# A new order of the first three periods, and 18 casts and copies on the other engine, in a hand-ordered fast matrix multiplication

## The chip, the cores and the metric

One core of a Trainium2 chip. The metric is the device time of one execution in microseconds (us). Five engines run their own queues of instructions side by side: TensorE (PE in the profile; its weight loads are PEld), VectorE (DVE), ScalarE (ACT), GpSimd (POOL) and SyncE (SP), which here issues every DMA. Semaphores order them against each other.

## The reference

```python
def setup_inputs():
    B, S, D = 8, 2048, 2048
    return {"x": randn(B, S, D), "w": randn(D, D)}          # float32

def reference(x, w):
    cs = np.cumsum(x, axis=1)
    diff = cs - np.concatenate([zeros, cs[:, :-1, :]], axis=1)
    return np.matmul(diff, w).astype(np.float32)
```

The differences of a running sum are x again, so the result is the product of x, read as 16384 rows of 2048, with w, 2048 x 2048. The kernel computes that product.

## The kernel before

The 16384 rows are 128 tiles of 128. Tiles 0 to 3 are multiplied plainly, in bf16, while w arrives. Tiles 4 to 127 go in groups of four (two "g" and two "h" tiles) by the Strassen-Winograd scheme: seven products of half-sized blocks in place of eight. Inside a group the products P1 to P5 are again done by seven quarter-sized products where the class `Quarters` is used (methods `one` to `four`, `middle`, `last`, and `slot(i)` for the i-th product), and plainly where `Whole` is used. Row tiles are scaled to fp16 ("narrow", with "weigh", "mean", "scale" and "unit" for the scale), transposed by DMA ("turn") and combined on VectorE ("S1g" and the like); w is scaled into blocks B11, B12, B21, B22 and combined into T1 to T4, and these into the operands of the inner products ("in1" to "in5").

**Periods.** Period 0 is everything up to and with the first group (`group_plain`, tiles 4 to 7); period 1 is `group` for tiles 8 to 11, period 2 for tiles 12 to 15, and so on to period 30; period 31 is the tail.

**The order is written out by hand.** No operation is issued where the code names it. `record(label, engine, ask)` collects it; `emit(places)` at the end sorts all 6670 of them by `period * 1620 + place`, where `places` is a dictionary from label to a number for periods 0, 1, 2, 29, 30 and 31, and one shared by all other periods, and issues them. `after` ties each instruction to the one before it on its engine, so the sorted order is each engine's queue order. A place may be negative: an operation of period 1 with place -1416 sorts among those of period 0. Waits between engines come from the data: a reader waits for its writer, and a writer for the readers of what it overwrites.

**The start** (period 0, labels as in the code). `first x.q.r` (256 KB each, line 254) and `w.h.ko` (512 KB each, line 295) are loaded through SyncE's queue. `cast x.q.a` makes x bf16 (line 260), `turn x.q.a` transposes it on TensorE by eight 128x128 operations into one PSUM bank (line 269), `turned x.q.a` copies that to SBUF (line 279). `turn x.0.0` uses bank 6 and every other one bank 7, so each of these waits until the bank was copied out. `cast w.h.ko` makes w bf16 in a ring of seven buffers (line 313), and `max w.h.ko` takes its largest magnitude (line 305). `plain.h.r.ko` are the products of row tile r with that w (line 324; two matmuls of 128x512, one for row tile 3 in half 0). `part.0` to `part.4` (line 376) and `part` (line 421) are that tile's other columns for ko below 5; `left over` (line 476) finishes them later from B11 and B21. `out.h.r.n` copies a result to SBUF (lines 340 and 342) and `put out...` stores it. 30 dummies `warm.0` to `warm.29` (line 362) multiply zeros before data is there; the zeros lie where `turned x.0.0` writes later. When all of w is in, `max`, `max of all`, `uw` and `uinv` give its scale, and the blocks `B11.k`, `B21.k` (line 460 on VectorE) and `B22.k` (line 462 on ScalarE) are scaled; `T1.k` is line 543.

**The groups.** `load`, `weigh` (line 140), `mean` (161), `scale` (163), `unit` (167), `narrow` (178) and `turn` (195) prepare a row tile. `keep C..` (line 624, ScalarE) copies a product out of PSUM with its scale into one of four result buffers, `C..+P..` (line 635, VectorE) adds to it, and `put` (line 643) stores it, which frees the buffer. `P1.first`, `P1.out2`, `P1.out4` and their like are copies by ScalarE (line 627), and all other sums are VectorE's (line 576). Matmuls are line 588 (a whole group of four) and line 610 (inner products).

In the code that the change replaces, the engine of an operation is fixed by its line: `cast x` on VectorE; `cast w`, `narrow`, `part`, `keep` and the copies on ScalarE; `turned` and `out` by an argument or a name. Which products of group 8 and later are inner sevens is decided by `all_seven(g)`, true from tile 12 on.

## Time and profile before

| | us |
|---|---|
| median of 3 runs | 1449.7 (1449.27 to 1450.26) |
| span of the profiled execution | 1449.2 |
| TensorE busy | 1438.6 |
| VectorE busy | 1334.3 |
| ScalarE busy | 1204.5 |
| GpSimd busy | 0.5 |

The span runs from the first to the last instruction of the profiled execution. A line of the timeline gives start and length in us, engine, source line, operation, tile written<-tiles read, shape, count of merged instructions, and in brackets the idle time of that engine just before and what ended it. A line by stage gives the stretch, its length, and for each engine its busy time and instruction count, then TensorE's granted clock, the mean busy share of the 16 DMA engines and the GB/s moved. SyncE's own line (SPq) shows the issue of DMAs, not their landing.

### The profile page before, as it was taken

To read this page: it belongs to the slowest core of one execution; us is meant where nothing else is said; L and a number is where in the kernel's file an instruction comes from. 1 tells how busy PE (TensorE), PEld (TensorE's weight loads), DVE (VectorE), ACT (ScalarE), POOL (GpSimd) and SP (SyncE) were. 2 spreads that over 40 slices of the span, in tenths; PEclk is the share of its full clock that TensorE was granted. 3 is DMA by queue.
4 is the path that set the end of the run, shared out by engine and by line. 5 is a ranking of instruction groups with operands and counts; after the bars stand their busy time and mean duration, and the time that the engine had idled before them with its cause. 6 is when DMAs were issued, how large, how long until landed. Compare 5 with 4: busy or idle time off the path is not lost.

```text
span 1449.2 us, 20358 instructions
## 1 busy us (share of the span) xinstructions
PE 1438.6 (99%) x6692; PEld 652.2 (45%) x6698; DVE 1334.3 (92%) x2345; ACT 1204.5 (83%) x1994; POOL 0.5 (0%) x5
## 2 busy tenths in 40 slices
PE   8999999999999999999999999999999999999998
PEld 4444444444444444444444444444444444444443
DVE  6999999999999999999999999999999999999988
ACT  5997888898888888888988888988888888889783
POOL 0000000000000000000000000000000000000000
PEclk9999999999999999999999999999999999999999
DMA  9999979899888999989998888998989998989973
GB/s 360 369 252 272 252 212 228 240 247 262 226 234 226 243 262 231 244 222 228 247 265 233 228 229 237 252 257 226 222 239 244 260 248 225 218 236 248 264 200 116
DMA packets 343930, 351.59 MB, mean 243 GB/s; under 512 B 270992, under 2 KB 270992, under 8 KB 343824
## 3 DMA queue, kind: packets, MB, share of 16 engines
q1 hardware_dynamic: 343824, 350.29, 89.4%
q8 instruction: 52, 0.85, 0.2%
q14 instruction: 54, 0.44, 0.1%
HBM read 150.99 MB, written 134.22 MB: 197 GB/s over the span
## 4 chain that ended last, share of the span: by engine, by line
PE 91%; issue 4%; DMA 2%; ACT 2%; DVE 1%; DVEq 0%; POOLq 0%; ACTq 0%; SPq 0%
PE b L610 61%; PE b L588 30%; DMA x<-F 1%; DMA F<-in_x_dram 1%; DVE W L460 1%; ACT waste L140 0%; DMA out_dram<-arena 0%; ACT W L462 0%; DVE arena L635 0%; ACT arena L624 0%; ACT F L178 0%; ACT arena L342 0%; ACT arena L178 0%; DVE arena L576 0%; DVE W L576 0%
## 5 line engine op out<-in xcount | busy, mean ns | idle before, releaser
L588 PE MATMUL b<-W,x 128*128 128x512 f16 x2144 | 518.1, 379 | 0.1
L635 DVE SCALAR_TENSOR_TENSOR arena<-b,tiny,arena 128x512 f32<-128x512 f32 x612 | 446.9, 745 | 16.0 <-PE b L610 4.8
L610 PEld LDWEIGHTS <-arena 128*128 128x128 f16 x2744 | 268.2, 98 | 325.4 <-DVE arena L576 6.3
L610 PE MATMUL b<-W,arena 128*128 128x512 f16 x1672 | 413.7, 379 | 0.8 <-DVE arena L576 0.4
L624 ACT ACTIVATE arena<-b,tiny 128x512 f32<-128x512 f32 x496 | 317.0, 684 | 35.4 <-PE b L588 14.9
L588 PEld LDWEIGHTS <-x 128*128 128x128 f16 x2144 | 209.7, 98 | 253.3 <-issue 0.3
L140 ACT ACTIVATE waste<-F,tiny 128x1024 uint8<-128x1024 f32 x246 | 283.9, 1154 | 15.6 <-DMA F<-in_x_dram 14.1
L178 ACT ACTIVATE F<-F,tiny 128x1024 f16<-128x1024 f32 x246 | 282.1, 1147 | 10.9 <-DVE tiny L163 9.4
L610 PE MATMUL b<-W,x 128*128 128x512 f16 x1192 | 287.5, 379 | 0.0
L610 PE MATMUL b<-arena 128*128 128x512 f16 x1072 | 261.6, 379 | 0.0
L610 PEld LDWEIGHTS <-x 128*128 128x128 f16 x1428 | 139.7, 98 | 168.5
L576 DVE TENSOR_TENSOR b<-b,arena 128x512 f32<-128x512 f32 x298 | 205.9, 691 | 5.7 <-ACT arena L627 2.0
L627 ACT COPY b<-b 128x512 f32<-128x512 f32 x149 | 85.5, 574 | 134.4 <-PE b L610 112.4
L627 ACT COPY arena<-b 128x512 f32<-128x512 f32 x298 | 170.2, 580 | 19.9 <-PE b L610 13.0
L576 DVE TENSOR_TENSOR arena<-W 128x2048 f16<-128x2048 f16 (+1 forms) x158 | 185.6, 1176 | 0.4 <-PE b L610 0.4
L576 DVE TENSOR_TENSOR arena<-x,x 128x512 f16<-128x512 f16 (+1 forms) x181 | 91.5, 506 | 50.1 <-PE b L610 50.1
L576 DVE TENSOR_TENSOR x<-x,x 128x1024 f16<-128x1024 f16 x124 | 85.2, 687 | 2.0
L576 DVE TENSOR_TENSOR arena<-W,arena 128x512 f16<-128x512 f16 (+1 forms) x157 | 85.9, 563 | 0.6 <-PE b L610 0.5
L576 DVE TENSOR_TENSOR arena<-arena 128x512 f16<-128x512 f16 x120 | 50.8, 424 | 13.7 <-PE b L610 11.8
L610 PE MATMUL b<-arena,x 128*128 128x512 f16 x236 | 60.3, 379 | 0.0
L324 PE MATMUL b<-arena 128*128 128x512 bf16 x234 | 53.5, 379 | 1.5 <-DVE arena L279 0.8
L576 DVE TENSOR_TENSOR arena<-x,arena 128x512 f16<-128x512 f16 x119 | 49.6, 417 | 0.6 <-PE b L610 0.6
(49 smaller groups left out, 503.6 us busy)
## 6 DMA issues: line engine op xcount, KB each, us to landing
F<-in_x_dram SPq DMA_DIRECT2D x246, 512.0 KB, 5.4
out_dram<-arena SPq DMA_DIRECT2D x240, 512.0 KB, 4.8
W<-in_w_dram SPq DMA_DIRECT2D x31, 512.0 KB, 9.5
out_dram<-arena SPq DMA_DIRECT2D x31, 256.0 KB, 2.7
W<-in_x_dram SPq DMA_DIRECT2D x16, 256.0 KB, 6.6
x<-F SPq DMA_TRANSPOSE x246, 4.4
arena<-in_x_dram SPq DMA_DIRECT2D x2, 512.0 KB, 5.1
W<-in_w_dram SPq DMA_DIRECT2D x2, 256.0 KB, 9.0
```

The lines of the kernel that those rows point to most:

```text
L140: lambda: nc.scalar.activation(waste, data, ABS, bias=least, scale=1.0 / ROW, accum_out=m),
L178: lambda: nc.scalar.activation(to, data, COPY, scale=s),
L324: said = nc.tensor.matmul(to[n], xP[:, r, ko, :], b[:, ds(n * NB, NB)], start=(ko == 0), stop=(ko == KO - 1),)
L460: ask = lambda: nc.vector.tensor_scalar(to, src, uinv, None, MUL)
L576: record(label, "dve", lambda: nc.vector.tensor_tensor(dst, p, q, op))
L588: said = nc.tensor.matmul(to[n], a[k], b[k][:, n, :], start=(start and k == 0), stop=(k == KH - 1), skip_group_check=True,)
L610: said = nc.tensor.matmul(to, a[k], b[k], start=(start and k == 0), stop=(k == 3), skip_group_check=True)
L624: record(label, "act", lambda: nc.scalar.activation(c, p, COPY, scale=u))
L627: record(label, "act", lambda: nc.scalar.copy(to, p))
L635: label, "dve", lambda: nc.vector.scalar_tensor_tensor(c, p, u, c, MUL, ADD)
```

## The change

The same operations are recorded, 6670 of them, with the same 6698 matmuls. Three things change.

1. **Places.** The dictionaries for periods 0, 1 and 2 are new; those of 29, 30, 31 and of all other periods are the same. TensorE's, VectorE's, ScalarE's and SyncE's queues are the same again from the last operations of period 2 on.
2. **Engines.** 18 operations go to the other engine, listed in `moved`. In period 0, from VectorE to ScalarE: `cast x.0.1`, `cast x.1.0`, `cast x.1.1`, `cast x.2.1`, `cast x.3.0`, `turned x.0.0`, `out.0.1.0`. From ScalarE to VectorE: `cast w.0.0`, `w.0.1`, `w.0.5`, `w.0.6`, `w.0.7`, `w.1.1`, `turned x.3.1`, `out.0.0.1`, `out.1.2.1`, and in period 2 `P3.first` and `narrow6.1`.
3. **Code around it.** `all_seven` becomes `plainly(name, g)`, and the making of inner operands goes through `made`; with the settings here the same products stay inner or plain as before.

Queues at the start, before:

```
PE:  warm.0-21, turn x.0.1, warm.22-28, turn x.1.0, warm.29, turn x.0.0, plain.0.1.0, plain.0.0.0, ...
DVE: zeros, least, ones, ..., cast x.0.1, turned x.0.1, cast x.1.0, cast x.0.0, cast x.1.1, turned x.0.0, max w.0.0, ...
ACT: cast w.0.0, turned x.1.0, cast w.0.1, cast w.0.2, cast w.0.3, cast w.0.4, turned x.1.1, ...
SP:  x.0.2, x.1.1, x.0.0, x.1.3, x.0.3, x.0.1, x.1.2, x.1.0, w.0.0, w.0.1, x.2.3, w.0.2, w.0.3, ...
```

and after:

```
PE:  warm.0-27, turn x.0.1, turn x.0.0, warm.28-29, turn x.1.0, plain.0.0.0, plain.0.1.0, plain.0.0.1, ...
DVE: ones, zeros, ..., cast x.0.0, least, cast w.0.0, turned x.0.1, cast w.0.1, max w.0.2, max w.0.3, ...
ACT: cast x.0.1, cast x.1.0, turned x.0.0, cast w.0.2, turned x.1.0, cast x.1.1, cast w.0.3, turned x.1.1, ...
SP:  x.1.1, x.0.1, x.0.2, x.0.3, x.0.0, x.1.0, w.0.0, w.0.1, w.0.2, x.1.3, x.1.2, w.0.3, w.0.4, w.0.6, ...
```

ScalarE's queue where period 1 begins, before and after (operations of period 1 marked):

```
before: ... P2.first(1), keep C21.1#2, weigh7.1, mean7, narrow7.0, narrow7.1, P2.out2(1), unit7, keep C21.0#2,
        weigh4.0(1), unit5, P2.out4(1), keep C11g.1(1), keep C11g.0(1), keep C11h.1(1), weigh4.1(1), mean4(1), keep C11h.0(1), ...
after:  ... P2.first(1), unit4, weigh7.0, weigh7.1, mean7, keep C21.0#2, narrow7.0, P2.out2(1), keep C21.1#2, narrow7.1,
        keep C11g.0(1), P2.out4(1), keep C11g.1(1), weigh4.0(1), keep C11h.0(1), unit7, keep C11h.1(1), weigh4.1(1), mean4(1), ...
```

The diff, cut to its core:

```diff
+    moved = {
+        0: (
+            "turned x.0.0", "cast w.0.0", "cast x.0.1", "cast w.0.1", "cast x.1.0",
+            "cast x.1.1", "cast x.2.1", "cast w.0.5", "cast w.0.6", "cast w.0.7", "cast x.3.0",
+            "turned x.3.1", "cast w.1.1", "out.0.0.1", "out.0.1.0", "out.1.2.1",
+        ),
+        2: (
+            "P3.first", "narrow6.1",
+        ),
+    }
+
     def record(label, engine, ask):
...
+        if isinstance(ask, dict):
+            if label in moved.get(period[0], ()):
+                engine = {"act": "dve", "dve": "act"}[engine]
+            ask = ask[engine]
         ops.append((period[0], label, engine, ask))
+
+    def on_two(to, src, scale=None):
+        if scale is None:
+            return {
+                "act": lambda: nc.scalar.copy(to, src),
+                "dve": lambda: nc.vector.tensor_copy(to, src),
+            }
+        return {
+            "act": lambda: nc.scalar.activation(to, src, COPY, scale=scale),
+            "dve": lambda: nc.vector.tensor_scalar(to, src, scale, None, MUL),
+        }
...
-        record(f"cast x.{q}.{a}", "dve", lambda: nc.vector.tensor_copy(to, src))
+        record(f"cast x.{q}.{a}", "dve", on_two(to, src))
...
-        record(f"cast w.{h}.{ko}", "act", lambda: nc.scalar.copy(to, src))
+        record(f"cast w.{h}.{ko}", "act", on_two(to, src))
...
     places = {
         0: {
-            'first x.0.2': 0, 'first x.1.1': 1, 'first x.0.0': 2, 'first x.1.3': 3,
-            'first x.0.3': 4, 'first x.0.1': 5, 'first x.1.2': 6, 'first x.1.0': 7, 'w.0.0': 8,
...
+            'ones': 1, 'first x.1.1': 1, 'zeros': 2, 'first x.0.1': 2, 'numbers': 3, 'warm.0': 3,
+            'first x.0.2': 3, 'numbers turned': 4, 'warm.1': 4, 'first x.0.3': 4, 'eye': 5,
...
```

More of the change, by code (lines that the diff above doesn't have):

```diff
@@ L277, in turned @@
         v = v.rearrange("p (r c) -> p r c", r=2)
-        on = nc.scalar.copy if engine == "act" else nc.vector.tensor_copy
-        record(f"turned x.{q}.{a}", engine, lambda: on(to, v))
+        record(f"turned x.{q}.{a}", engine, on_two(to, v))
     wb = {}
@@ L420 @@
                 part(k)
-            record("part", "act", lambda: nc.scalar.copy(partial, banks[7]))
+            record("part", "act", on_two(partial, banks[7]))
     for ko in range(KO - KQ, KO):
@@ L815, in slot, with plainly, made @@
                 matmuls(*halves_of(f"{self.name}{name}", to, a, self.right, True)[at % 4])
+    def plainly(name, g):
+        return name in {PLAIN + 4: ('P1',)}.get(g, ())
+    making = {}
+    def made(name, inner, how):
+        if name not in making:
+            making[name] = True
+            how(inner)
     def group_plain(g):
@@ L972, in group @@
         P1.slot(1)
-        if more:
+        if not P1.plain:
             in_1.give("Q4")
@@ L1015, in group @@
         P1.slot(6)
-        if not more:
-            make_5(in_5)
-        in_5.give("Q3")
+        if not P5.plain:
+            made("P5", in_5, make_5)
+            in_5.give("Q3")
         C11h = keep("keep C11h", Y, uh, free.pop(1))
@@ L1033, in group @@
         total("S4g", S4g, A12g, S2g, SUB)
-        if not more:
-            make_1(in_1)
+        if not plainly("P1", g + 4):
+            made("P1", in_1, make_1)
+        if not plainly("P2", g + 4):
+            made("P2", in_2, make_2)
         go(2)
@@ L1055, in group @@
         P5.slot(4)
-        in_3.give("Q1")
+        if not P3.plain:
+            in_3.give("Q1")
         P5.last()
@@ L1101, in group @@
         P3.last()
-        in_4.give("Q1")
+        if not P4.plain:
+            in_4.give("Q1")
         scale_of(next_k)
@@ L1162, in group @@
         P4.slot(6)
+        if P4.plain and not plainly("P4", g + 4):
+            made("P4", in_4, make_3)
+        if P5.plain and not plainly("P5", g + 4):
+            made("P5", in_5, make_5)
+        if P3.plain and not plainly("P3", g + 4):
+            made("P3", in_3, make_3)
         turn(next_l, [1])
```

70 lines of the change are left out of this document (33 added, 37 removed), and 460 rows, old and new, of the table places.

## The prediction

> **What bounds the kernel now.** I read the page's first part, then busy time by stage, then the timeline of the stages that the change touches. From the page:
>
> ```profile
> span 1449.2 us, 20358 instructions
> PE 1438.6 (99%) x6692; PEld 652.2 (45%) x6698; DVE 1334.3 (92%) x2345; ACT 1204.5 (83%) x1994; POOL 0.5 (0%) x5
> ```
>
> The span is 1449.2 us and the median of the runs 1449.7, so 0.5 us lies around the span; sums are made in the span and the 0.5 added at the end. TensorE is busy for 99%. By stage (start:end, length, busy time of PE, PEld, DVE, ACT and POOL with instruction counts, clock, DMA share, GB/s):
>
> ```profile
> 0.00:13.20 13.20, 9.56 (x55) 4.49 (x55) 6.24 (x16) 2.91 (x3) 0.19 (x4) 1.00 0.82 284
> 13.20:41.00 27.80, 27.54 (x153) 13.53 (x157) 21.48 (x21) 22.14 (x25) 0.00 (x0) 1.00 1.03 405
> 41.00:118.00 77.00, 76.20 (x350) 34.15 (x352) 75.69 (x120) 68.57 (x100) 0.35 (x1) 1.00 1.01 304
> 118.00:146.00 28.00, 27.16 (x126) 12.05 (x124) 26.39 (x61) 22.93 (x40) 0.00 (x0) 1.00 1.02 258
> 146.00:1400.00 1254.00, 1254.00 (x5811) 568.17 (x5810) 1162.46 (x2061) 1064.45 (x1789) 0.00 (x0) 1.00 0.90 238
> ```
>
> From 146 to 1400 us PE has no idle time at all: 1254.00 us for 5811 matmuls, 0.2158 each. The change touches the first three periods, which end early in this last stage, and issues the same matmuls, so it can win only what PE idles before 146 us: 3.64 in the first stage (much of it the first load's latency), then 0.26, 0.80 and 0.84. In return any wait that the new order puts in front of PE costs its full length. A matmul's record is 0.379 long while the next follows after 0.216, so an idle time that the view prints is 0.16 shorter than the delay behind it; I add 0.16 below.
>
> **Part 1, the start.** Rows of the timeline (start, length, engine, line, operation, count, idle time before it and what ended it):
>
> ```profile
> 1.17 6.24 PE L362 MATMUL b<-arena 128*128 128x512 bf16 x22 [1.17 <-DVE arena L237]
> 8.34 0.69 DVE L260 CAST W<-W 128x1024 bf16<-128x1024 f32 x1 [5.08 <-DMA W<-in_x_dram]
> 9.09 0.62 PE L269 MATMUL b<-waste,W 128*128 128x128 bf16 x8 [1.68 <-DVE W L260]
> 9.55 1.68 PE L362 MATMUL b<-arena 128*128 128x512 bf16 x7
> 9.75 0.69 DVE L279 COPY arena<-b 128x1024 bf16<-128x1024 bf16 x1 [0.72 <-PE b L269]
> 10.37 1.90 DVE L260 CAST W<-W 128x1024 bf16<-128x1024 f32 x3
> 11.57 1.05 ACT L313 CAST arena<-W 128x1024 bf16<-128x1024 f32 x1 [9.57 <-DMA W<-in_w_dram]
> 12.52 1.01 ACT L279 COPY arena<-b 128x1024 bf16<-128x1024 bf16 x1
> 13.19 4.30 PE L324 MATMUL b<-arena 128*128 128x512 bf16 x17 [0.79 <-DVE arena L279]
> 16.09 1.04 ACT L313 CAST arena<-W 128x1024 bf16<-128x1024 f32 x1 [0.23 <-DMA W<-in_w_dram]
> 17.37 1.04 ACT L313 CAST arena<-W 128x1024 bf16<-128x1024 f32 x1 [0.23 <-DMA W<-in_w_dram]
> ```
>
> The two casts that end on DMA at 16.09 and 17.37 show the pace of loads: 1.28 per 512 KB tile, 0.64 per x block of half that size. Before, w.0.0 is the ninth load, behind eight x blocks, and lands just ahead of the cast at 11.57. After, it is the seventh, behind six: 1.28 earlier, so its cast can start at 10.29. That cast goes to VectorE (0.69 in row 8.34, against 1.05 on ScalarE) and ends at 10.98; `turned x.0.1` waits behind it in VectorE's queue and ends about 0.69 later, 11.67. `turn x.1.0` needs the PSUM bank that this copy empties: 11.74, with 0.45 for its eight transposes, and `plain.0.0.0` starts at 12.2. The other branch is earlier: `cast x.0.1` on ScalarE ends near 8.8 (its later block is the fourth load instead of the fifth: 8.34 less 0.64, plus 1.05), the 28 leading dummies end near 8.5 (row 1.17's end plus six of 0.216), `turn x.0.0` (behind `cast x.0.0`, 8.34 + 0.69, and `turn x.0.1`) and two more dummies end near 10.3, and `turned x.0.0` on ScalarE, 1.01, by 11.4. So the first product moves from 13.19 to 12.2: **gain 1.0**. The dummies themselves cost nothing: all lie before data is there.
>
> **Part 2, 13 to 41 us.** PE now runs ahead of the loads.
>
> ```profile
> 24.33 4.60 DVE L305 TENSOR_REDUCE tiny<-W 128x1 f32<-128x1024 f32 x4 [0.70 <-DMA W<-in_w_dram]
> 41.84 4.48 PE L324 MATMUL b<-arena 128*128 128x512 bf16 x19 [0.34 <-ACT arena L313]
> ```
>
> The reduction at 24.33 waits for the 20th load (w.0.8), after 7 MB. In the new order the 20th load, after the same 7 MB, is w.0.7. Its cast, on VectorE, ends at 24.33 + 0.69 = 25.0. PE needs it for `plain.0.3.7`: 52 matmuls (11.2) and two sets of transposes (0.9) behind 12.2 make 24.3. A wait of 0.8 appears, with about 0.2 more from the other tiles. The idle of the same stage before is 27.80 - 27.54 = 0.26 as printed, and up to 0.16 more for each wait in it: I take 0.7 for several short ones, between 0.26 and 0.9, and let it go. Net **-0.3**. The wait of 0.34 + 0.16 at 41.84, for `cast w.1.1` on ScalarE, goes too: that cast moves to VectorE and its tile comes one place earlier: **+0.5**. Ahead by 1.2 at 42 us.
>
> The 18 engine moves in themselves: an SBUF cast costs 0.69 on VectorE and 1.05 on ScalarE, `turned` 0.69 and 1.01 (rows 9.75 and 12.52); the two `out` copies about 0.1 more on VectorE than on ScalarE, by these rows:
>
> ```profile
> 40.27 0.58 ACT L342 COPY arena<-b 128x512 f32<-128x512 f32 x1
> 40.52 0.68 DVE L340 COPY arena<-b 128x512 f32<-128x512 f32 x1
> ```
>
> No row has `P3.first` (PSUM to PSUM) or `narrow6.1` on VectorE. The nearest are the subtraction from PSUM to PSUM and the scaling of SBUF:
>
> ```profile
> L627 ACT COPY b<-b 128x512 f32<-128x512 f32 x149 | 85.5, 574 | 134.4 <-PE b L610 112.4
> L576 DVE TENSOR_TENSOR b<-b,arena 128x512 f32<-128x512 f32 x298 | 205.9, 691 | 5.7 <-ACT arena L627 2.0
> L178 ACT ACTIVATE F<-F,tiny 128x1024 f16<-128x1024 f32 x246 | 282.1, 1147 | 10.9 <-DVE tiny L163 9.4
> 61.04 2.74 DVE L460 TENSOR_SCALAR W<-W,tiny 128x1024 f16<-128x1024 f32 x4
> ```
>
> I take 0.69 and, from the pace of row 61.04, 0.75: +1.4 of VectorE's time in period 2. From 146 us on VectorE has 1254.00 - 1162.46 free, 7%, so 20 us absorb it. Cost 0; the ends are 0 and +1.4 if it all meets PE. The Trainium skill ("VectorE: DVE Perf Modes", Specifications) puts VectorE closer to SBUF and ScalarE closer to PSUM, by which all four PSUM reads that go to VectorE would lose; the trace agrees for f32 (0.68 against 0.58) and not for bf16 `turned` (0.69 against 1.01). By the page the sum would be under 1 us worse on an engine with that slack, and the same on PE.
>
> **Part 3, 41 to 118 us.** All of w must be there before B11 is scaled, so this start is set by loads, not by PE:
>
> ```profile
> 56.69 2.96 ACT L313 CAST arena<-W 128x1024 bf16<-128x1024 f32 x3 [0.31 <-DMA W<-in_w_dram]
> 69.07 0.81 PE L476 MATMUL b<-W,arena 128*128 128x512 f16 x3
> 86.10 1.25 PE L588 MATMUL b<-W,arena 128*128 128x512 f16 x5 [0.25 <-DVE arena L576]
> ```
>
> The cast at 56.69 waits for w.1.13; w.1.14 follows 1.28 later, 57.9, last in both orders. So the scaling that starts at 61.04 stays there or comes up to 0.7 earlier, if VectorE is less behind with its reductions. `left over.0` comes 1.2 earlier, 67.9, and `A11g B11.0.0` at 68.5; B11.0 is now eleventh of the blocks and ready at 61.04 + 10 x 0.66 + 0.07 + 0.75 = 68.5: just in time. At 86.10 PE waits for `S1g` (0.25 + 0.16). In the new order two T2 blocks fall behind `S1g` and one `out` ahead of it, 0.6 sooner, while PE comes 1.2 sooner: the wait becomes 0.2 to 1.0, by how early the scaling starts; I take 0.3, since the reductions of w.0 all fit in VectorE's early gaps (21.48 busy of 27.80 in stage two). **+0.1**, and 0.1 more from smaller waits. Ahead by 1.4 at 118 us.
>
> **Part 4, 118 to 146 us.** This is where the sum is open.
>
> ```profile
> 129.72 0.58 ACT L627 COPY arena<-b 128x512 f32<-128x512 f32 x1 [0.48 <-PE b L610]
> 131.00 1.84 ACT L624 ACTIVATE arena<-b,tiny 128x512 f32<-128x512 f32 x3 [0.70 <-DMA out_dram<-arena]
> 132.97 1.03 PE L610 MATMUL b<-arena,x 128*128 128x512 f16 x4
> 133.35 1.15 ACT L140 ACTIVATE waste<-F,tiny 128x1024 uint8<-128x1024 f32 x1 [0.51 <-DMA F<-in_x_dram]
> 136.99 1.02 PE L610 MATMUL b<-W,arena 128*128 128x512 f16 x4 [0.40 <-ACT b L627]
> 138.45 1.90 PE L610 MATMUL b<-W,arena 128*128 128x512 f16 x8 [0.44 <-DVE arena L576]
> ```
>
> Before, ScalarE waits at 133.35 for load8.1 with `keep C11h.0` behind it; that delays VectorE's `C11h+P2.h`, and PE waits 0.56 and 0.60. After, `keep C11h.0` is ahead of that `weigh4.1`, so these 1.16 go. But `keep C11g.0`, which at 131.00 waits for a store (put3.1) to free its buffer, is now ahead of `P2.out4` (129.72) in ScalarE's queue. Behind `P2.out4` stand `P2.6` on PE and, on VectorE, `P2.last`, `S2g` and `S1h`. With the store at 131.0, `P2.out4` would end at 131.0 + 0.57 + 0.58 = 132.1. `P2.6` (132.97) stands one group of four (0.86) earlier in the new order and PE is 1.4 ahead: 130.7, a wait of 1.4. `P2.last` (0.69) and `S2g` (0.68) come only then, while PE has one group to do: 0.9 with the reaction times; `S1h` and the P5 sums behind them make 0.7 more. About 3.0. If the store lands by 129, `P2.out4` ends by 130.2 and only 0.3 of the last is left. It stands one place earlier in SyncE's queue (before load8.0), which is worth one tile, 1.28; so I take a landing near 130 and a wait of 1.6. Net 1.16 - 1.6 = **-0.4**, between +0.9 and -1.8.
>
> Sum: 1.0 - 0.3 + 0.5 + 0.1 + 0.1 - 0.4 = 1.0. After 146 us PE and VectorE find their old order again by period 3; I book 0. Span 1448.2, time **1448.7**.
>
> **The rivals.**
>
> *The store lands early.* Nothing takes the place of the 1.16: 1.4 + 0.9 = 2.3, so 1447.4. For it: the store's earlier place. Against it: at its end the rate of this stretch falls to what one DMA engine of 16 moves, and one instruction fetch lies in it; I read this as the fetch holding one engine back, and the fetch comes again.
>
> ```profile
> GB/s 197 262 131 229 295 197 262 328 262 229 197 197 229 295 229 295 328 328 328 426 426 360 361 338 391 369 340 246 272 240 207 172 137 104 72 33 45 33 33 33
> q8 instruction: 1, 0.02, 1.5%
> ```
>
> These are 127 to 132 us: the rate sinks from 426 to 33, a thirteenth. The Trainium skill ("Runtime: NRT & Kernel Launch", Instruction fetch mechanics) calls the cost of a fetch mostly hidden; by that the store lands without delay and this rival is right. Chance 0.27.
>
> *Every wait goes*, also w.0.7's and S1g's: 2.3 + 1.0 + 0.3 = 3.6, 1446.1. It needs loads faster than the rows show; chance 0.10.
>
> *Slower: ScalarE's queue behind the store.* Place: `keep C11g.0` ahead of `P2.out4`. Price: 3.0 at a landing of 131.0, and 1 us for each later. At 131.0 the sum is 1.4 + 1.16 - 3.0 = -0.4, 1450.1; it decides from a landing of 130.6. For slower by more than 0.2% (2.9 us) the store must land after 133.5. Chance 0.18 in all, 0.08 beyond 2.9.
>
> *It does not start earlier*: the first loads set the pace whatever the order, `plain` starts at 13.19 again and the rest nets to zero: 1449.7. Chance 0.10; the seventh place of w.0.0 speaks against it.
>
> **How the numbers follow.** Forecast 1448.7, chance 0.35; the others 0.27, 0.10, 0.18 and 0.10. A measurement of this kernel tells about 0.2% (2.9 us: 1446.8 to 1452.6) from no change. Faster by more: the "every wait goes" case and a little of the early store, 0.13. Slower by more: 0.08 from the store. Within: 0.79. The range of 8 in 10 takes in the early store, half of "every wait goes" and the store at 132: 1446.4 to 1451.2.
>
> **What would show it.** Right: L324's first matmul near 12.2; a PE wait near 25 ended by a VectorE cast; none at 41.8; ScalarE's L624 after 125 us with a wait on out_dram and PE idle right after it; no idle from 146 us. Wrong: first L324 at 13 or later, idle time of PE in periods 1 and 2 ended by VectorE (P3.first, narrow6.1), or PE idle near 68.5 for B11.

## The result, and the profile after

The changed kernel takes 1455.64 us (median of 5 runs, 1453.49 to 1457.7) against 1450.26 (1449.27 to 1450.42) for the kernel before beside it: the ratio is 1.0035, 95% interval 1.0023 to 1.0047. It is slower by 0.2 to 0.5%, and its runs spread over 4 us, those of the kernel before over 1.

The first part of the page after:

```profile
span 1452.6 us, 20366 instructions
PE 1439.5 (99%) x6691; PEld 652.6 (45%) x6698; DVE 1336.9 (92%) x2349; ACT 1201.0 (83%) x1990; POOL 0.5 (0%) x5
```

The work of every engine is the same within 4 us; the span is 3.4 longer. So the time has to be looked for where TensorE waits. By stage, after:

```profile
41.00:118.00 77.00, 74.85 (x344) 33.52 (x346) 74.60 (x115) 66.67 (x97) 0.35 (x1) 1.00 1.03 300
118.00:146.00 28.00, 28.00 (x131) 12.74 (x130) 27.81 (x67) 22.76 (x40) 0.00 (x0) 1.00 0.99 283
146.00:1400.00 1254.00, 1251.74 (x5797) 566.85 (x5796) 1161.20 (x2058) 1060.19 (x1784) 0.00 (x0) 1.00 0.91 238
```

From 41 to 118 us TensorE idles 2.15 instead of 0.80; from 118 to 146 not at all, instead of 0.84; and from 146 us on, where it never idled, 2.26. The view of waits says for whom (waiting tile and line, what it waited for, us in all, times, longest). After:

```profile
PE b L600 <- DMA x<-F: 1.9, 2, 1.4
PE b L622 <- ACT b L140: 1.7, 3, 0.7
PE b L291 <- DVE arena L141: 1.6, 1, 1.6
PE b L378 <- DVE arena L259: 1.3, 1, 1.3
PE b L345 <- DVE arena L141: 0.5, 1, 0.5
PE b L622 <- ACT arena L144: 0.4, 1, 0.4
```

and the same view of the kernel before:

```profile
PE b L269 <- DVE W L260: 1.7, 1, 1.7
PE b L362 <- DVE arena L237: 1.2, 1, 1.2
PE b L324 <- DVE arena L279: 0.8, 1, 0.8
PE b L610 <- DVE arena L576: 0.4, 1, 0.4
PE b L610 <- ACT b L627: 0.4, 1, 0.4
...
```

One kind is new: a wait for the DMA that transposes a row tile (`x<-F`). Another has grown: waits for ScalarE's copies between PSUM banks and out of them (L140 and L144; casts and copies now share these lines, since a helper issues them) are 2.1 us in four waits, where the kernel before had one of 0.4 (L627).

To compare places I sum, over the matmuls, the start-to-start time beyond 0.216 us (0.055 for a transpose), leaving out gaps of exactly one matmul that is missing from the trace. This lateness of TensorE, in us, at points of equal work, in the profiled executions of four kernels (E13 and E16 are experiments below):

| about | 70 us | 85 us | 122 us | 143 us | 184 us | 271 us | end |
|---|---|---|---|---|---|---|---|
| before | 6.82 | 6.82 | 7.28 | 8.45 | 8.46 | 8.47 | 8.80 |
| after | 6.19 | 8.70 | 8.70 | 8.70 | 9.55 | 11.88 | 12.20 |
| E13 | 5.87 | 6.18 | 6.49 | 6.49 | 7.74 | 9.17 | 9.80 |
| E16 | 6.10 | 6.33 | 6.64 | 6.64 | 7.01 | 7.02 | 7.40 |

After gains 0.6 by 70 us, loses 2.5 by 85 us, gains 0.5 and 1.2 by 143 us, and loses 0.8 and 2.3 behind it: 3.4 in all. (This profiled execution took 1454.4 us, 1.2 less than the median. In the profiled executions of all 18 experiments 1.8 us, in one 2.0, lie between the span and the time of the same execution, with either start; by that the profiled execution of the kernel before took about 1451, an estimate. So the two profiles are 3.4 apart and the medians 5.4, and these pieces explain the profiles; which waits make the median longer still is not shown.)

**The start.** Timeline of VectorE, then of TensorE, after:

```profile
11.31 0.69 DVE L141 CAST arena<-W 128x1024 bf16<-128x1024 f32 x1 [2.72 <-DMA W<-in_w_dram]
11.92 0.68 DVE L141 COPY arena<-b 128x1024 bf16<-128x1024 bf16 x1
```

```profile
12.66 0.61 PE L291 MATMUL b<-waste,W 128*128 128x128 bf16 x8 [1.58 <-DVE arena L141]
...
25.93 0.81 PE L345 MATMUL b<-arena 128*128 128x512 bf16 x3 [0.53 <-DVE arena L141]
```

`cast w.0.0` waits for its load until 11.31, `turned x.0.1` stands behind it, `turn x.1.0` behind that: the first product starts at 13.1, where it started at 13.19 before.

**The middle.** SyncE's queue after (its own line; the length is that of the issue):

```profile
64.79 1.35 SPq L217 DMA_TRANSPOSE x<-F  x1
66.20 1.53 SPq L362 DMA_DIRECT2D out_dram<-arena  x3
67.83 1.01 SPq L529 DMA_DIRECT2D arena<-in_x_dram  x2
68.97 6.35 SPq L217 DMA_TRANSPOSE x<-F  x2
75.75 0.83 SPq L362 DMA_DIRECT2D out_dram<-arena  x2
76.64 1.08 SPq L158 DMA_DIRECT2D F<-in_x_dram  x2
77.81 1.25 SPq L217 DMA_TRANSPOSE x<-F  x1
```

and before:

```profile
55.33 6.66 SPq L346 DMA_DIRECT2D out_dram<-arena x6
...
65.06 1.34 SPq L195 DMA_TRANSPOSE x<-F  x1
66.51 0.99 SPq L517 DMA_DIRECT2D arena<-in_x_dram  x2
67.61 1.25 SPq L195 DMA_TRANSPOSE x<-F  x1
68.91 0.60 SPq L132 DMA_DIRECT2D F<-in_x_dram  x1
70.05 2.54 SPq L195 DMA_TRANSPOSE x<-F  x1
...
```

Between `turn0.0` and `turn0.1` there now stand three stores, and two more between `turn2.0` and `turn2.1`; before, all five went out ahead of `turn0.0` (one at 52.81 us, four among the six issued from 55.33), while SyncE had to wait for `narrow0.0` anyway. `turn0.1` lands at 76.78 instead of 73.67, `turn2.1` at 84.27 instead of 79.35. TensorE, after:

```profile
76.82 0.60 PE L600 MATMUL b<-W,x 128*128 128x512 f16 x2 [1.45 <-DMA x<-F]
...
84.31 1.04 PE L600 MATMUL b<-W,x 128*128 128x512 f16 x4 [0.41 <-DMA x<-F]
```

**The late part.** ScalarE's timeline after:

```profile
168.86 1.15 ACT L166 ACTIVATE waste<-F,tiny 128x1024 uint8<-128x1024 f32 x1 [0.92 <-DMA F<-in_x_dram]
...
170.01 0.57 ACT L140 COPY b<-b 128x512 f32<-128x512 f32 x1
...
233.23 0.69 ACT L144 ACTIVATE arena<-b,tiny 128x512 f32<-128x512 f32 x1 [1.87 <-DMA out_dram<-arena]
...
240.22 0.59 ACT L140 COPY b<-b 128x512 f32<-128x512 f32 x1
```

and TensorE's:

```profile
170.64 1.02 PE L622 MATMUL b<-W,x 128*128 128x512 f16 x4 [0.68 <-ACT b L140]
...
217.01 1.02 PE L622 MATMUL b<-arena 128*128 128x512 f16 x4 [0.37 <-ACT b L140]
...
233.97 1.02 PE L622 MATMUL b<-W,x 128*128 128x512 f16 x4 [0.39 <-ACT arena L144]
...
240.87 1.02 PE L622 MATMUL b<-W,arena 128*128 128x512 f16 x4 [0.70 <-ACT b L140]
```

Each time ScalarE's queue stands still behind one instruction that waits for a DMA, and a copy that TensorE needs is queued behind it. At 168.86 it is `weigh7.1`, which waits for `load7.1`, with `P1.first` behind it; the wait at 217.01 has the same form one period later (`load7.1` lands at 214.83); at 233.23 it is `keep C12g.0`, which waits for the store `put-1.0` to free its buffer (landed at 233.20; 229.18 before), and then everything up to `P3.first` at 240.22 is late.

### The profile page after: what moved, and what is told of

Its sections match the earlier page's. It is cut to its first block, busy times and chain, and to the rows that moved or that the text cites. A ratio compares the mean times of both kernels' runs of the same rounds, so it can differ in the third digit from the quotient of the medians.

```text
span 1452.6 us, 20366 instructions
## 1 busy us (share of the span) xinstructions
PE 1439.5 (99%) x6691; PEld 652.6 (45%) x6698; DVE 1336.9 (92%) x2349; ACT 1201.0 (83%) x1990; POOL 0.5 (0%) x5
## 4 chain that ended last, share of the span: by engine, by line
PE 94%; DMA 3%; ACT 1%; DVE 1%; SPq 1%; issue 0%; DVEq 0%; ACTq 0%
PE b L622 60%; PE b L600 31%; PE b L345 3%; DMA W<-in_w_dram 1%; DMA out_dram<-arena 1%; DMA arena<-in_x_dram 1%; DMA x<-F 0%; DMA F<-in_x_dram 0%; ACT arena L144 0%; SPq L276 0%; ACT F L144 0%; DVE arena L647 0%; ACT waste L166 0%; ACT arena L140 0%; DVE b L588 0%
## 5 line engine op out<-in xcount | busy, mean ns | idle before, releaser
L647 DVE SCALAR_TENSOR_TENSOR arena<-b,tiny,arena 128x512 f32<-128x512 f32 x612 | 447.7, 746 | 16.3 <-PE b L622 4.7
L144 ACT ACTIVATE arena<-b,tiny 128x512 f32<-128x512 f32 x496 | 318.0, 684 | 39.5 <-PE b L600 18.7
L144 ACT ACTIVATE F<-F,tiny 128x1024 f16<-128x1024 f32 x245 | 280.9, 1146 | 8.9 <-DVE tiny L189 7.6
L140 ACT COPY arena<-b 128x512 f32<-128x512 f32 (+1 forms) x316 | 182.8, 588 | 20.9 <-PE b L622 14.0
L140 ACT COPY b<-b 128x512 f32<-128x512 f32 x148 | 84.9, 574 | 133.3 <-PE b L622 112.3
```

What stands on the lines that cost most here:

```text
L140: "act": lambda: nc.scalar.copy(to, src),
L144: "act": lambda: nc.scalar.activation(to, src, COPY, scale=scale),
L647: label, "dve", lambda: nc.vector.scalar_tensor_tensor(c, p, u, c, MUL, ADD)
```

## The experiments

Theory: the loss is one of order, in two places, and each time a transfer comes late in SyncE's queue: stores among the transposes of period 0, and the order of periods 1 and 2. Rivals: the engine moves; the late place of ScalarE's table load; the late part inherited from the early one; slower transfers by chance. All times are medians. Ratios are to the kernel before run beside each; they are taken over all runs and are not the quotient of the two medians.

### E1: three of the stores ahead of `turn0.0`

```diff
-'put out.0.0.0': 155, ... 'put out.0.2.1': 156, ... 'put out.0.3.0': 157,
+'put out.0.0.0': 150, ... 'put out.0.2.1': 150, ... 'put out.0.3.0': 150,
```

> Queue theory: in the changed kernel three stores (put out.0.0.0, out.0.2.1, out.0.3.0) stand between turn0.0 and turn0.1 in SyncE's queue, so turn0.1 lands at 76.78 us (73.67 before) and turn2.1 at 84.27, and PE waits 1.4 and 0.4 us for them (1.61 and 0.58 with the 0.16 and 0.22 that a printed idle time hides). With the three stores ahead of turn0.0, where SyncE idles from 56.5 to 64.8 us, turn0.1 should land near 73.7 and both waits go: 2.2 us less up to 118 us, time near 1453 if nothing later takes it back. Rival (the transpose is late because of the loads and of itself, not of the stores): both waits stay, time unchanged at 1454 to 1456. Second rival (drift: transfers were slower in the one profiled execution): the waits change in every run, also where the order is unchanged.

1452.44 us, ratio 1.0018 (1.0009 to 1.0027). The wait for `turn0.1` fell from 1.61 to 0.26; that for `turn2.1` stayed (0.73). `turn0.1` landed at 74.80, not at 73.7. Stores matter. That more than these three do is read from the landings and waits; E13 takes it up.

### E2 and E7: `P1.first` and `weigh7.1`

E2 takes `P1.first` ahead of `weigh7.1`, and with it past `C22h+Y.0`, whose bank it overwrites, so a part of group 1's result is another; E7 moves `weigh7.1` behind `P1.first` instead.

```diff
-'P1.first': -2882,
+'P1.first': -2884.5,
```
```diff
-'weigh7.1': -1264,
+'weigh7.1': -1261.5,
```

> Queue theory: P1.first of period 2 stands behind weigh7.1 in ScalarE's queue, and weigh7.1 waits for load7.1 (landed 168.78 us), so PE's P1.3 waits 0.84 us at 170.6. With P1.first one place earlier, ahead of weigh7.1, that wait goes: 0.8 less, 1453.6 to 1454.8. The waits near 76.8 and 84.3 (2.2 us) and those at 217 to 244 us (2.2 us) stay. Rival (PE is simply early, and the next wait takes over): the wait moves to P2.first or P1.out2, 0.5 us or more of it, and the time stays. Drift theory: the waits at 76.8 and 217 to 244 us, which this edit doesn't touch, change by more than 0.5 us.

> Only weigh7.1 of period 1 goes behind P1.first of period 2 in ScalarE's queue (the edit that was meant before, without taking P1.first past C22h+Y.0). Queue theory: the wait of PE at 170 us (0.84 us in the changed kernel, 1.02 and 1.20 in two others with this order) goes, since P1.first no longer stands behind an instruction that waits for load7.1; time 0.8 to 1.0 lower, 1454.6 to 1454.9, and with 0.3 of it lost again where mean7 and narrow7 come later. Rival (P1.first is late because of C22h+Y.0 on VectorE, which ends at 167.2 and whose bank it overwrites): the wait stays above 0.5 us.

E2: 1456.91, ratio 1.0047 (1.0034 to 1.006), with 2.3 us of waiting at 171 us, for VectorE: the wait became longer, not shorter. E7: 1454.6, ratio 1.0036 (1.0024 to 1.0049). In E7 the wait at 170 us is gone, but waits of 0.19, 0.26 and 0.79 stand at 182 to 189 us: `narrow4.0` and `P5.first` of the next period are now behind. (E7's profiled execution, 1458.36 us, also has a wait of 2.5 at 86.6 for `turn2.1`, which the edit doesn't touch.) One operation less in front moves the wait and doesn't remove it; the rival with the next wait was right.

### E3: the moves of period 2 undone

```diff
-        2: ("P3.first", "narrow6.1"),
+        2: (),
```

> Only the two engine moves of period 2 are undone (P3.first and narrow6.1 back on ScalarE), with the new order kept. Moves theory: the 1.44 us that they add to VectorE (0.70 and 0.74 in the trace) put C22g+X.1, and so put2.1, load7.0 and load7.1 behind it in SyncE's queue, later, and by that come the four waits at 217, 234, 241 and 244 us (2.2 us): they go, time 2.0 to 2.4 lower, 1452.5 to 1453.5. Order theory (the new place of C22g+X.1 behind in4.Q3, P4.middle and C12h+Y.1 makes put2.1 late): the waits stay within 0.7 us of 2.2 and the time is the same.

1456.87, ratio 1.0046 (1.0032 to 1.006). The waits stay (1.20, 0.70, 0.38, 0.86, 0.29), and new ones of 2.18 us (2.0 in print) and 0.40 appear at 198 and 185 us. Both theories on record expected the same time or less. The view of waits of E3, first line (L134 is the shared copy's line here):

```profile
PE b L616 <- ACT b L134: 4.5, 5, 2.0
```

The moves theory falls: in this order the two moves cost nothing, and without them there is a wait more. In the trace after they take 0.70 and 0.74 us on VectorE. The order theory holds for the old waits, but did not foresee the new ones.

### E4, E10, E12, E9: the two orders joined at a seam

Operations up to a seam are issued in one order, the others in the other order, with the engines that belong to each:

```diff
     def when(op):
         at, label = op[:2]
+        if label in early.get(at, ()):
+            return early[at][label] - 10000
...
-    emit(places)
+    emit(places, early)
```

> The new order is kept for everything ahead of S3g T3.0.0 of period 1 (146 us), and all that follows comes in the order and on the engines of the kernel before. Theory (the loss behind 146 us, 3.1 us, is the order and the moves of the second half of period 1 and of period 2): no wait of PE from 146 to 1400 us but up to 0.5 at the seam, time 3.1 less, 1451.0 to 1452.5, with the waits at 76.8 and 84.3 still there. Rival (the loss behind 146 us is inherited: the first 146 us leave loads and stores late, and that delays periods 2 and 3 whatever their order): at least 1.5 us of waits appear between 146 and 260 us again, time 1453 or more.

1452.52, ratio 1.0019 (1.0011 to 1.0028): no wait from 150 to 1400 us, but 1.95 at the seam, on VectorE, where at most 0.5 was expected. The two waits of the middle stayed (0.99 and 0.56).

> The new order up to P4.last of period 2 (170 us), the order and engines of the kernel before behind it (so P3.first and narrow6.1 on ScalarE). Late theory in two parts: the wait at 170 us belongs to period 1's order and stays (0.8 to 1.2), those from 215 to 245 us belong to period 2's order and go (2.2 in the changed kernel's profile). Time 2.2 lower: 1453.0 to 1453.6. Rival (the later waits follow from the one at 170 us and from late loads): at least 1 us of waits remains between 180 and 250 us.

1453.64, ratio 1.0023 (1.0013 to 1.0033): 2.03 us of waiting at 171, at the seam, and none from 172 to 800 us. So the waits from 215 to 245 us come with the order of period 2 behind that seam, and aren't inherited.

> Order and engines of the kernel before up to A11g B11.0.1 of the first group (72 us), the new order and the moves behind it (out.1.2.1, P3.first, narrow6.1). The cut lies where the two orders have issued nearly the same operations. Three parts are put to the test. Start theory: what the changed kernel loses outside the span (1.8 us there against 0.5) and in its loads belongs to the order of the first loads, so here 0.5 us lie outside and w.0.0 lands at 11.55 as before. Middle theory: the waits at 76.8 and 84.3 us come from the stores ahead of turn0.1, so they go. Late theory: the waits at 170 us (0.8 to 1.0) and 215 to 245 us (1.2 to 2.2) belong to the order of periods 1 and 2 and come back. Sum: 1450.1 + 0.9 + 1.7 - 1.2 (the two waits at 137 and 138 us of the kernel before go) = 1451.5. Rival (the late waits are inherited from the late start): none of them, 1449.

1452.27, ratio 1.0012 (1.0003 to 1.0021). No wait from 42 to 168 us; at 169 us 1.21, at 238 us 0.86 and 0.30. The middle and the late part came as expected. The start did not: w.0.0 landed at 12.21, and 1.8 us lay outside the span with the old start too, so that these 1.8 are no part of the change.

> The reverse: the new order and engines up to the same operation, the order of the kernel before behind it. Start theory: 1.7 to 1.9 us outside the span, w.0.0 at 11 or later. Middle theory: turn0.1 is already behind the three stores, so PE's wait near 76.8 us (1.0 to 1.6) stays. Late theory: no wait at 170 nor from 215 to 245 us; the waits at 137 and 138 us (1.2) are back. Sum: 1450.1 + 1.3 (outside) + 1.5 (middle) = 1452.9, with the first 70 us equal within 0.4. Rival (inherited): waits of 1.5 us or more behind 146 us, 1454 or more.

1458.48, ratio 1.0055 (1.0043 to 1.0068), 5.6 above the forecast. From 112 to 1400 us all waits were below 0.1, as the theory has it. But the seam put an `out` copy in ScalarE's queue behind a store that the new order issues late (7.1 us of ScalarE, 4.2 of TensorE at 85 us). The middle wait stood as forecast (1.43 at 76.6 us), and behind the long wait the granted clock was 0.5 until 88 us (last section). A seam is an order of its own, and the time of this one shows nothing about the middle.

### E5 and E8: the start

```diff
+    record("table", "act", lambda: nc.scalar.copy(tiny[:, 65:66], zeros[:, :1]))
```
```diff
-'cast w.0.0': 11,
+'cast w.0.0': 32.5,
```

> One ScalarE copy of a single column is added at the very start; it waits only for the zeros (0.98 us), not for a load. In the changed kernel ScalarE's first instruction is cast x.0.1, which waits for two loads, and the table load (1.28 us) stands behind the first of these waits, at 7.0 us; in the kernel before it stands at 0.72. Table theory: with the table load early again, (a) cast x.0.1 starts near 7.0 instead of 8.3, (b) the stretch in which the fifth to eighth half-megabyte of loads lands is no longer slowed, so w.0.0 lands near 10.3 instead of 10.95 to 12.06 as in the five executions with this start, and the first product starts near 12.2 instead of 13.1, and (c) the 1.8 us between the span and the time of the same execution falls to the 0.5 of the kernel before. Time 2.0 to 2.5 lower than the changed kernel's 1455.6: 1453.0 to 1453.7. Rival (the loads are slow at the start by themselves, and the 1.3 us outside the span have to do with something else, for instance with two more instructions): w.0.0 lands at 11 or later, 1.8 us stay outside the span, time 1455 to 1456.

1453.46, ratio 1.0031 (1.0019 to 1.0042). The table load went from 7.0 to 0.7 us, and nothing else happened: w.0.0 landed at 11.51, the first product started at 13.3, 1.8 us lay outside the span. The median lies in the band that the table theory forecast, but by luck: none of its three steps came, and the ratio can't be told from the changed kernel's 1.0035. The table theory falls.

> Only cast w.0.0 goes behind turned x.0.1 in VectorE's queue. Chain theory for the start: turned x.0.1 no longer waits for w.0.0's landing and ends near 11.0, turn x.1.0 follows at once, and the first product waits for cast w.0.0 and turned x.0.0, which both end near 12.1: it starts near 12.2 instead of 13.1, 0.9 earlier. PE then runs 0.9 further ahead of the loads, and the wait at 25.9 us (0.69) grows by about as much: at 42 us no more than 0.3 of the gain is left, time 1455.3 to 1455.6. Rival (loads do not bound this stretch): the gain stays, the wait at 25.9 keeps its length, time 1454.7.

1455.59, ratio 1.0034 (1.0021 to 1.0046). The first product started at 12.45, but waits of 0.43, 0.68 and 0.55 at 13.7, 17.2 and 26.2 us took the gain back. The chain theory was right: in this order of the loads TensorE can't get ahead of the loads.

### E6: table, three stores and `weigh7.1` together

> The early table load, the three stores ahead of turn0.0, and weigh7.1 behind P1.first in ScalarE's queue, together. If the three causes are separate: 1455.6 less 2.3 (table), less 3.2 (stores, as measured alone) and less 0.8 (weigh7.1): 1449.3, no longer different from the kernel before. If the table load and the stores work by the same delay: 1451 or more.

1454.12, ratio 1.0026 (1.0016 to 1.0037): not the sum. `turn0.1` landed at 76.55 with the three stores ahead as well (wait 1.21), and with `weigh7.1` moved back, waits of 2.1 us in all stood between 174 and 192 us.

### E11 and E13: the transpose first, or all five stores first

```diff
-'put out.0.0.0': 155, ... 'turn0.1': 170,
+'put out.0.0.0': 155.3, ... 'turn0.1': 155.2,
```
```diff
-'put out.0.0.0': 155, 'put out.0.2.1': 156, 'put out.0.3.0': 157, 'put out.0.1.1': 175, 'put out.0.2.0': 176,
+'put out.0.0.0': 150, 'put out.0.2.1': 150, 'put out.0.3.0': 150, 'put out.0.1.1': 150, 'put out.0.2.0': 150,
```

> The changed kernel with turn0.1 directly behind turn0.0 in SyncE's queue, ahead of the three stores and of load1.0 and load1.1. Queue theory: turn0.1 lands near 70 instead of 76.8, before TensorE's instruction fetch near 74 us slows one DMA engine; the wait at 76.8 goes entirely (1.0 to 1.6 in the runs with this order). Chain theory (rival): the stores and loads that are now behind it come later, turn2.0 and turn2.1 with them, and the wait at 84.3 us grows by as much: the sum of both waits stays near 2.2 and the time at 1455.6. If only the first theory holds: 1454.0 to 1454.5.

1456.21, ratio 1.0038 (1.0025 to 1.0052). The wait at 76.8 went, and one of 2.71 stood at 79.1 for `turn2.0`. The chain theory was right: what counts is all that stands in front of the transposes together, not the place of one.

> The changed kernel with all five late stores of half 0 (put out.0.0.0, 0.2.1, 0.3.0 and also 0.1.1, 0.2.0) ahead of turn0.0, as in the kernel before; with three of them moved, turn0.1 still landed at 74.80 and turn2.1 at 82.45 us (73.67 and 79.35 before), and 0.26 and 0.73 us of waits were left. Store theory: the two that still stood between turn2.0 and turn2.1 hold the rest, so turn2.1 lands near 80 and the waits from 66 to 85 us, 2.2 to 2.5 us in the changed kernel, fall below 0.5; time 2 to 3 lower, 1452.6 to 1453.6. Rival (the transposes are late because of an instruction fetch of TensorE at 70 to 74 us that slows one DMA engine, and of the loads): 1 us or more of waits stay, 1454 or more.

1452.04, ratio 1.0017 (1.0007 to 1.0026): 0.18% less than the changed kernel, 2.6 us by the ratios. Beside E14, which ran with it and kept the stores where they were (1455.02), ten of its eleven runs (1451.06 to 1452.87) lie below the lowest of E14's (1453.79). `turn0.1` landed at 74.18 and `turn2.1` at 81.41. The view of waits of E13 and its SyncE queue:

```profile
PE b L622 <- ACT b L140: 1.8, 2, 1.1
PE b L291 <- DVE arena L141: 1.4, 1, 1.4
PE b L378 <- DVE arena L259: 1.3, 1, 1.3
PE b L345 <- DVE arena L141: 0.4, 1, 0.4
```

```profile
64.49 1.34 SPq L217 DMA_TRANSPOSE x<-F  x1
65.96 1.18 SPq L529 DMA_DIRECT2D arena<-in_x_dram  x2
67.64 4.76 SPq L217 DMA_TRANSPOSE x<-F  x2
```

No wait for `x<-F` is left. The store theory holds for the five stores together. By time E13 can't be told from E1 with three of them (1452.44), and E6, with the same three, still had a wait of 1.21; that the last two matter rests on these waits.

Slower transfers by chance do not explain this part: in the nine other profiles in which three stores stand between `turn0.0` and `turn0.1` as in the changed kernel (E2, E3, E4, E5, E7, E8, E10, E12, E14), TensorE waits 0.9 to 1.5 us for `turn0.1`, and in E13, E16 and E17, with all five stores ahead, not at all.

### E14 and E17: the late store of period 2

E17 has the five stores of E13 as well.

```diff
-'C22g+X.1': -2813,
+'C22g+X.1': -2816.5,
```
```diff
-'put2.1': -2813, 'load7.0': -2812, 'load7.1': -2811,
+'load7.0': -2816.9, 'load7.1': -2816.8, 'put2.1': -2813,
```

> The changed kernel with one VectorE operation of period 2 earlier: C22g+X.1 directly behind P4.s3 instead of behind C12h+P3.h.1, P4.middle and C12h+Y.1, so that put2.1, and with it load7.0 and load7.1 behind it in SyncE's queue, are issued about 1.3 us earlier. Late-store theory: load7.1 and put-1.0 of period 3 land more than 1 us earlier, keep C12g.0 no longer waits for its buffer, and the waits from 215 to 245 us (2.2; in all runs with this order 0.86 and 0.29 at least) go down to 0.5 or less. Rival (what delays period 3 is not this store but the whole order of period 2's second half): the 0.86 and the 0.29 stay, and the time is the same, 1455 to 1456.

1455.02, ratio 1.0035 (1.0022 to 1.0048). `put2.1` went out at 206.64, no earlier: it stores C12h and waits for `C12h+Y.1`, which the edit made later. My reading was wrong; 0.86 and 0.29 stayed, and a wait of 0.6 at 206.7 is new.

> The kernel with the five stores ahead of turn0.0, and besides load7.0 and load7.1 of period 2 ahead of put2.1 in SyncE's queue. The look at C22g+X.1 was aimed at the wrong operation: put2.1 stores C12h and waits for C12h+Y.1, which ends at 206.0 us in the changed kernel (203.4 before), and SyncE stands still behind it from 202.2 us on, with load7.0 and load7.1 ready to go at 202.3 and 203.5. Queue theory: load7.1 lands at 211 to 212.5 instead of 214.8, all that follows it in SyncE's queue comes 2 us or more earlier, put-1.0 of period 3 lands before 231.5 instead of 233.2, keep C12g.0 does not wait for its buffer, and of the waits from 214 to 245 us (1.4 in the run with the five stores: 0.25, 0.85, 0.29) less than 0.4 is left; time 1 lower than with the five stores alone (1452.0): 1450.9 to 1451.2. Rival (the whole order of period 2): the 0.85 and 0.29 stay, 1451.6 to 1452.4.

1451.78, ratio 1.0013 (1.0003 to 1.0022), no difference from E13 that can be told. `load7.1` landed at 208.5 (212.7 in E13) and the wait at 215 us was gone, but `put-1.0` landed no earlier (231.9, 230.5 in E13; TensorE was 1.9 late at 170 us here), and 0.48 and 0.29 stayed at 240 us. Half a hit: two loads are one part of it, and the rest lies in the order of period 2 as a whole.

### E15 and E16: the gaining part alone, and both repairs

E15: the old order up to 72 us, the new one to `S3g T3.1.1` of period 1 (157 us), the old one behind it. E16: the new order to that operation with the five stores of E13, the old one behind it.

> The part of the new order that gained, alone: the order of the kernel before up to 72 us, the new order from there to S3g T3.1.1 of period 1 (157 us), the order of the kernel before behind it; of the moves only out.1.2.1 is left. Theory: the waits at 137 and 138 us of the kernel before (1.2) and its wait at 86 us (0.4) go, none comes at 170 or behind 215 us, and the seam costs at most 0.3: 1.2 to 1.6 faster than the kernel before, 1448.6 to 1449.0. Rival (the gain is taken back at the next wait of the loads, or by the seam): equal to the kernel before within 0.4.

1449.65, ratio 0.9997 (0.9988 to 1.0006): no difference from the kernel before, where 1.2 to 1.6 us less were forecast; the rival was right. The waits at 137 and 138 us were gone in its profile, and 0.47 at 76 us new.

> Both repairs together: the new order and its moves up to S3g T3.1.1 of period 1 (157 us) with the five stores ahead of turn0.0, and the order and engines of the kernel before behind that. If the middle waits and the late waits are all that the change loses, both are gone, and what the new order gains up to 60 us (0.5 to 1.5) and at 137 us (1.2) is left: 1448.0 to 1449.5. Rival (a loss that I have not found, common to all kernels with the new start): 1450.5 or more.

1449.6, ratio 0.9998 (0.9989 to 1.0007). The view of waits of E16:

```profile
PE b L287 <- DVE arena L135: 2.1, 1, 2.1
PE b L374 <- DVE arena L255: 1.3, 1, 1.3
PE b L341 <- DVE arena L135: 0.5, 1, 0.5
PE b L618 <- DVE b L584: 0.2, 1, 0.2
PE b L287 <- ACT W L134: 0.2, 1, 0.2
```

Neither a wait for `x<-F` nor one for ScalarE's copies is left. With both repairs the whole loss is gone, so no third one shows: 0.35% is 0.18 (the stores, E13) and 0.19 (the second half of period 1 and period 2, E13 to E16), less 0.02. All of E16's runs (1448.88 to 1450.41) lie below E13's lowest, 1451.06. E16 keeps all 16 engine moves of period 0, so in this order they cost no more than the new order gains. Neither E15 nor E16 beats the kernel before by more than the measurement tells, though E16's lateness is 1.4 us less in the profiles.

### E18: the 18 moves alone, in the old order

> The 18 engine moves alone, in the order of the kernel before. Theory (the loss is all in the order; a cast costs 0.69 on VectorE against 1.05 on ScalarE, and both engines have room at the start): within 0.5 of the kernel before, 1449.5 to 1450.5, with P3.first on VectorE in period 2 adding no wait. Rival (the moves only pay with the order made for them, and cost without it, since an operation lands in the other engine's queue at a place that nobody chose): 1451 or more, with waits of PE in the first 70 us or near 193 us.

1479.7, ratio 1.0206 (1.0192 to 1.0219). VectorE's timeline in E18:

```profile
46.94 17.57 DVE L328 TENSOR_REDUCE tiny<-W 128x1 f32<-128x1024 f32 x16
...
68.27 0.69 DVE L141 CAST arena<-W 128x1024 bf16<-128x1024 f32 x1
```

`cast w.1.1`, needed by TensorE near 47 us, takes its place in VectorE's queue by the old numbers, behind 16 reductions, the scale and four scaled blocks: TensorE waits 21.8 us at 69.0. The theory was wrong and its rival right. This wait is the greater part of the 29.7 us; others are 2.7 at 16.3, 1.7 at 32.7 and 0.7 at 222.2 (for `P3.first` on VectorE, which in this order does add a wait), and behind the two longest the granted clock was 0.5 for some us (last section). The moved casts were not slower (0.69 on VectorE, 1.05 on ScalarE); a move is a place in another queue, and the price lies in that place.

## Why the prediction was wrong, point by point

- **What bounds the kernel**: right as far as it went. TensorE's waits are the matter; the busy time of the engines hardly changed.
- **Part 1, the start, +1.0**: wrong in one number. The chain was as described (load, cast, `turned x.0.1`, `turn x.1.0`), but "1.28 earlier for two places" took the pace of the loads as fixed. That step failed: w.0.0 landed at 11.29 instead of 10.29 (10.95 to 12.06 in the runs with this start, 11.17 to 12.21 in the four with the old one). First product at 13.1; gain 0.1. The rival "it does not start earlier" was right about the start, and not about the rest, which it let net to zero.
- **Part 2, +0.2**: the wait of 0.8 near 25 us came (0.69, ended by a VectorE cast), the one at 41.84 went. At 70 us after is ahead by 0.6 instead of 1.2. That `P3.first` and `narrow6.1` cost nothing in this order held (E3); the moves of period 0 were not undone in the new order, and E16 bounds them.
- **Part 3, +0.2**: this step failed. The S1g wait went, as half expected, and `A11g B11.0.0` was in time. But I followed VectorE's blocks and never walked SyncE's queue, where five stores had moved in among the transposes. It lost 2.5 us in the profile; E13 shows 2.6 by the ratios.
- **Part 4, -0.4**: wrong to the good side. `put3.1` landed at 129.1, no wait came: the rival with the early store.
- **"After 146 us ... I book 0"**: this step failed too, a term put at nothing without a walk along the queues, and is as large: 3.2 us in the profile, 2.8 by the ratios of E13 and E16. That TensorE had no idle time there before was read as slack. It was a property of the old order; periods 1 and 2 had a new one, and I didn't follow their queues.
- **The slower rival** had a chance of 0.08 for more than 0.2%, and only if `put3.1` landed after 133.5. It named the right mechanism (ScalarE's queue standing behind a store, with a copy that TensorE needs behind it), with the wrong address: not `keep C11g.0` at 131 us but `keep C12g.0` at 233, and `weigh7.1` behind a load at 169 and 215.
- **The signs of being wrong**: the late start came (13.1). The others looked at VectorE and at B11; the waits that decided came from a DMA and from ScalarE, which none of them named. "No idle from 146 us", a sign of being right, failed.
- **0.5 us around the span**: the span was of one execution, the median of others. It is 1.8 where both are of the same one. This shifts no difference, but should not have been in the sum.

The sum with measured terms, from the table: +0.63 (to 70 us), -2.51, +0.46, +1.17, -0.84, -2.32 makes -3.4 where the forecast had +1.0.

What stays open: which operations of period 2's order make `put-1.0` late (E17 found a part), why the sixth and seventh load of the new start are slow, how much of E1's and E6's difference is the fetch named below, and what makes the changed kernel's median 1.2 us longer than its profiled execution.

## What to carry to other kernels

When an order written by hand is changed, walk every queue from the first moved operation to the last one, the DMA queue first: for each instruction that waits for a transfer, list what is queued behind it and who needs that. A stretch in which the bounding engine never idles says that the old order fits, not that there is room for a new one. And a change of engine is a change of queue: judge it by the place at which the operation lands, not by its duration.

## What the runs showed that I had not expected

- **A transpose by DMA landed behind all that was issued ahead of it, and the queue stood nearly still before that.** DMA traffic of the changed kernel from 73.5 to 77 us, in 40 slices:

```profile
GB/s 287 255 167 257 339 135 91 70 18 18 6 0 0 0 0 6 6 9 9 12 9 9 9 12 44 272 295 287 293 258 284 284 298 290 287 293 290 293 290 284
q8 instruction: 1, 0.02, 1.7%
```

  From 74.2 to 75.6 us hardly anything moves, though `turn0.1` (issued at 68.97) and more are queued. The packets of a transpose have 256 bytes each; in the trace's packet records half of `turn0.1` starts between 73.0 and 74.4, and 20 of these packets stay open until 75.7. One 16 KB instruction fetch runs from 73.94 to 74.88, and from 74.86 to 75.68 packets go one at a time. `load1.1`, next ahead of `turn0.1`, lands at 75.90, and `turn0.1` at 76.78. This fits a fetch that holds one DMA engine back while the others wait for it, but that is only argued: the records don't name the engine, and no run moved the fetch alone. A like hole stands in the kernel before (0 to 82 GB/s from 74.8 to 76.1, ahead of `turn2.0`), and there TensorE waits for no transpose. The Trainium skill ("Runtime: NRT & Kernel Launch", Instruction fetch mechanics) calls the cost of a fetch mostly hidden; no run here shows what the fetch costs, only that after the change the hole ends in a wait of TensorE.
- **The issue of the second of two transposes can hold SyncE**: it took 3.84 us at 71.48 and 4.41 at 220.70, where the first took 1.24 and 1.30, and ended shortly before the load ahead of both had landed (75.32 and 75.90, 225.11 and 225.28). In E13 it took 1.23.
- **The first loads don't keep a fixed pace.** From the fifth landing on, 768 KB took 2.0 us in the kernel before (8.24 to 10.28) and 3.5 in the changed one (7.79 to 11.29), 2.1 to 5.0 in the runs with this start and 1.9 to 2.7 in those with the old one. The early table load (E5) didn't change it. The cause is open.
- **A table load takes the place of its engine's first wait.** With `cast x.0.1`, which waits for two loads, as ScalarE's first instruction, it ran at 7.0 instead of 0.72 us; by time this cost nothing that could be told (E5).
- **A long wait of TensorE can cost more than its length.** In the profiled executions of E2, E7, E10 and E18 the granted clock fell to 0.5 for 3.41 us, in or shortly behind a wait of 2.3, 2.5, 4.2 and 2.7 us, and in E18 for 20.48 us around its long one. Matmuls then follow each other every 0.427 us instead of 0.216, which cost about 1.5 us more. In E11 a wait of 2.7 us left the clock at 1.0, so the length alone does not decide.
